# Ranks to keys with the heads innermost, a bf16 tree in place of a reduce, and another order of score and U products

## The chip, the cores and the metric

The kernel runs on one core of a Trainium2 chip. The metric is device time in microseconds, from one launch of the kernel; lower is better. Five engines work side by side, each on its own queue in order: TensorE (PE), VectorE (DVE), ScalarE (ACT), GpSimd (POOL) and SyncE (SP), which issues most of the transfers.

## What is computed

One layer of an encoder on 512 tokens of 1024 features: a mixer (a recurrence and a convolution behind one projection), then PEER, a retrieval over 128 x 128 experts, and a last norm. The change lies in PEER:

```python
def retrieve(xt):                                     # 128 tokens
    q = einsum("td,de->te", xt, w_q).reshape(128, 8, 2, 128)
    s = einsum("thpc,hpkc->thpk", q, sub_keys)        # 8 heads, 2 halves, 128 keys
    s1, i1 = top_k(s[:, :, 0], 16)
    s2, i2 = top_k(s[:, :, 1], 16)
    cand_s = s1[..., :, None] + s2[..., None, :]      # 16 x 16 pairs
    cand_i = i1[..., :, None] * 128 + i2[..., None, :]
    top_s, pos = top_k(cand_s, 16)                    # of the 256
    idx = take_along_axis(cand_i, pos)
    gate = softmax(top_s)
    act = gelu(einsum("thkd,td->thk", expert_u[idx], xt))
    return einsum("thk,thkd->td", gate * act, expert_v[idx])
```

## The kernel before

All matrix products on float32 data are made from two halves: a value is split into `hi` (a cast on ScalarE, line 108) and `lo` (a subtraction on VectorE or GpSimd, line 110), and three products are summed (`hi` by `hi`, `hi` by `lo`, `lo` by `hi`). `split` takes its buffers from a pool of three, so at most three weight tiles are split ahead of TensorE; `load` (line 101) takes one of five raw tiles of 512 KB and issues its transfer on SP's queue.

The first 128 x 3 tokens are treated densely: all 128 x 128 experts are multiplied (`u_t`, 128 chunks of U; then `v_t`, 128 chunks of V), and a gate matrix, mostly zeros, weighs them between. The last 128 tokens gather their chosen rows. The order in time is:

1. The mixer, which leaves its normed output in `m_hi` and `m_lo`, one block of 128 tokens after another (`turn`, line 134; the last block's transposes come last). A product of one U chunk (`dense_u`, line 457) reads the first 384 tokens, a query (`query`, line 562) all 512.
2. The retrieval (lines 551 to 592). For each of 16 half-heads `hp`: a query product of 24 matmuls, copied to SBUF (line 571); the scores `p_s` (line 581, eight matmul passes), copied to `s` (line 584); `rank` (line 495), five ranking instructions on VectorE for each block of 128 tokens, which leave the 16 best values and their indices in `v16` and `i16`. U products stand between them to fill TensorE: `EARLY` two ahead of the first query, one after every half-head from 1 to 14, six after the last, 22 in all. After half-heads 3, 7 and 11 `choose` (line 502) treats a pair of heads, after 13 and 15 one head.
3. `choose`: `ii` is a bf16 copy of the indices (line 510, ScalarE); the candidates' sums `cs` (line 514); their 16 best, `ts` at `pos` (line 522, two rounds of eight for each head and block); the two ranks `pb` out of the position (lines 528 to 534). Then, for each of the two keys, the index at that rank: a compare of the rank with all 16 numbers, `ioj` (line 537), a product with `ii` (line 539), and a reduce over the 16 (line 541) into `key_d`. The gates are a softmax (lines 544 to 549: GpSimd, ScalarE, VectorE, GpSimd).
4. The scatter (lines 603 to 662). `turned` (line 603) transposes gates and keys of one block, so that (head, key) lies on the partitions; for each group of `GS` = 8 tokens VectorE makes two one-hots (line 634) of the two keys and three products with the gate's three bf16 parts (line 638), and TensorE multiplies them to 128 x 128 gates a token (line 644), which go out to `scr_g` (line 648). After each 16 tokens (24 times) one more U product is made, as long as fewer than 46 are done.
5. The V stage (from line 728): each chunk of U is weighed with its gates and multiplied with its chunk of V (line 745), while the other 128 tokens' rows are gathered.

A scheduler of the framework sets the final order of instructions on each engine; instructions of neighbouring steps are seen interleaved in the trace, above all the rankings.

Of the kernel before, what the change touches and what calls it, by code (L numbers as in the profile page):

```python
# [18 lines left out]
P = 128  # L19
# [41 lines left out]
def tile_kernel(ctx, tc, x, par, wi, bd, kd, mg, wo, wq, keys, u_rows, v_rows, u_t, v_t, fg, ffg, sel, out):  # L61
# [382 lines left out]

    AHEAD_U = 51
    AHEAD_W = 2
    EARLY = 2
    us = {}

    HOMES = AHEAD_U + 1 - 8  # L450
# [26 lines left out]
    for _ in range(4):  # L477
# [21 lines left out]
    def merge(t):  # L499
        return t.rearrange("p h b k -> p (h b) k")  # L500

    def choose(rp, v, i, g, keys_, h0, n):

        hh = slice(h0, h0 + n)
        vv = v[:, hh].rearrange("p h b t k -> p (h b) t k")
        m = vv.shape[1]
        shp = [P, m, K]
        big = [P, K, m, K]
        ii = rp.tile([P, m, 2, K], BF16, name="ii")
        nc.scalar.copy(ii, i[:, hh].rearrange("p h b t k -> p (h b) t k"))  # L510

        cs = rp.tile([P, m, NCD], F32, name="cs", bufs=1)
        for lo_, ni, nj, c0 in ((0, 4, K, 0), (4, 12, 4, 64)):
            (nc.gpsimd if n > 1 else nc.vector).tensor_tensor(
                cs[:, :, c0:c0 + ni * nj].rearrange("p h (i j) -> p h i j", j=nj),
                vv[:, :, 0, lo_:lo_ + ni].unsqueeze(3).to_broadcast([P, m, ni, nj]),
                vv[:, :, 1, 0:nj].unsqueeze(2).to_broadcast([P, m, ni, nj]), op=ALU.add)
        ts = rp.tile(shp, F32, name="ts")
        pos = rp.tile(shp, U32, name="pos")
        for h in range(m):  # L520
            c2 = rp.tile([P, NCD], F32, name="c2")
            best16(ts[:, h], pos[:, h], cs[:, h], c2)

        pa = rp.tile([P, 5, m, K], U32, name="pa")
        for q, (op, arg) in enumerate(((ALU.logical_shift_right, 4), (ALU.logical_shift_right, 2),
                                       (ALU.bitwise_and, 15), (ALU.bitwise_and, 12),
                                       (ALU.logical_shift_right, 6))):
            nc.vector.tensor_scalar(pa[:, q], pos, arg, None, op0=op)
        pf = rp.tile([P, 5, m, K], F32, name="pf")
        nc.scalar.copy(pf, pa)  # L530
        pb = rp.tile([P, 2, m, K], BF16, name="pb")
        nc.vector.scalar_tensor_tensor(pb[:, 0], pf[:, 1], -12.0, pf[:, 0], op0=ALU.add, op1=ALU.max)
        nc.vector.tensor_mul(pf[:, 3], pf[:, 3], pf[:, 4])
        nc.vector.tensor_sub(pb[:, 1], pf[:, 2], pf[:, 3])
        for t in range(2):
            eq = rp.tile(big, BF16, name="eq")
            nc.vector.tensor_tensor(eq, pb[:, t].unsqueeze(1).to_broadcast(big), ioj[:, :, 0:m, :],  # L537
                                    op=ALU.is_equal)
            nc.vector.tensor_tensor(eq, eq, ii[:, :, t, :].rearrange("p h j -> p j h").unsqueeze(3)  # L539
                                    .to_broadcast(big), op=ALU.mult)  # L540
            nc.vector.tensor_reduce(merge(keys_[:, t, hh]), eq.rearrange("p j h k -> p h k j"),  # L541
                                    axis=AX.X, op=ALU.add)
        g = merge(g[:, hh])
        nc.gpsimd.tensor_tensor(g, ts, ts[:, :, 0:1].to_broadcast(shp), op=ALU.subtract)
        nc.scalar.activation(g, g, AF.Exp)
        den = rp.tile([P, m], F32, name="den")
        nc.vector.tensor_reduce(den, g, axis=AX.X, op=ALU.add)
        nc.vector.reciprocal(den, den)
        nc.gpsimd.tensor_tensor(g, g, den.unsqueeze(2).to_broadcast(shp), op=ALU.mult)

    with ExitStack() as rt:
        kp = rt.enter_context(tc.tile_pool(name="kp", bufs=1, side="right"))
        ky = kp.tile([P, 16, NK], F32, name="ky")
        nc.sync.dma_start(ky, keys)
        rp = rt.enter_context(tc.tile_pool(name="rp", bufs=2, side="right"))
        qp = rt.enter_context(tc.tile_pool(name="qp", bufs=4, side="right"))
        ps_q = rt.enter_context(tc.tile_pool(name="ps_q", bufs=3, space=PSUM))
        ps_s = rt.enter_context(tc.tile_pool(name="ps_s", bufs=3, space=PSUM))
# [44 lines left out]
    def turned(b):  # L603

        tr = bp.tile([P, P], F32, name="tr", bufs=1)
        trb = bp.tile([P, 5, P], BF16, name="trb", bufs=2)
        for dst, src in ((tr, gate_d[:, :, b]), (trb[:, 0], key_d[:, 0, :, b]), (trb[:, 1], key_d[:, 1, :, b])):
# [4 lines left out]
            nc.scalar.activation(dst, p, AF.Copy)  # L612
        for q in range(2, 5):
            nc.scalar.copy(trb[:, q], tr)
            if q < 4:
                nc.vector.tensor_sub(tr, tr, trb[:, q])
        return trb

    def scatter(b, trb):
# [3 lines left out]
        for t0 in range(0, P, GT):  # L623
            stg = bp.tile([P, NK, GT], F32, name="stg", bufs=2)
            for t1 in range(0, GT, GS):

                def over(q):
                    return (trb[:, q, t0 + t1:t0 + t1 + GS].rearrange("p (g t) -> p g t", t=SB).unsqueeze(2)
                            .to_broadcast(shp))

                hot = []
                for q in (0, 1):
                    o = bp.tile(shp, BF16, name=f"hot{q}", bufs=2)
                    nc.vector.tensor_tensor(o, iot.unsqueeze(1).to_broadcast(shp), over(q), op=ALU.is_equal)  # L634
                    hot.append(o)
                oa = bp.tile([P, 3] + shp[1:], BF16, name="oa", bufs=2)
                for q in range(3):
                    nc.vector.tensor_tensor(oa[:, q], hot[1], over(2 + q), op=ALU.mult)  # L638
                for t2 in range(0, GS, 4):
                    p = ps_g.tile([P, 4, NK], F32, name="p_g")  # L640
                    for t in range(4):
                        g, o = divmod(t2 + t, SB)
                        for q in range(3):
                            nc.tensor.matmul(p[:, t, :], hot[0][:, g, :, o], oa[:, q, g, :, o],  # L644
                                             start=(q == 0), stop=(q == 2))
                    o = t1 + t2
                    nc.scalar.activation(stg[:, :, o:o + 4], p.rearrange("p t k -> p k t"), AF.Copy)
# [213 lines left out]
```

## Time and profile before

| | us |
|---|---|
| median of 3 runs (1582.27 to 1582.92) | 1582.82 |
| the profiled execution | 1580.88 |
| its span, first to last instruction | 1579.1 |

| engine | busy us | share of the span |
|---|---|---|
| TensorE, matmuls | 1479.1 | 94% |
| TensorE, weight loads | 1299.8 | 82% |
| VectorE | 1234.1 | 78% |
| ScalarE | 634.8 | 40% |
| GpSimd | 639.4 | 40% |

Times of day are microseconds from the span's start. Busy time is an average over stages; a stage is read by its own stretch. Matmuls are pipelined and their ends are modelled, so the distance from start to start tells what one costs. "[idle before <-X]" names what ended an engine's idle time.

### The profile page before, as it was taken

Reading aid. Unit: us, or ns where it says so; the run is one execution under the profiler, and the core shown is the slowest. Engines: PE = TensorE matmul, PEld = TensorE weight load, DVE = VectorE, ACT = ScalarE, POOL = GpSimd, SP = SyncE. Lnnn points to the kernel's source line nnn. Section 1 sums busy time; section 2 is a strip of 40 time slices with the busy share of each in tenths; the row PEclk is TensorE's granted clock in tenths of the full one; section 3 lists DMA queues with packets and bytes.
Section 4 is the critical chain, followed back from the end, with each engine's and each line's share of the span. In section 5 each row is a group of like instructions: output and inputs, shape, how many; then the busy total and the mean of one; then the engine's idle time right before and its main releaser. Section 6 shows DMA issues by size and latency. Waiting matters only on the chain.

```text
span 1579.1 us, 21654 instructions
## 1 busy us (share of the span) xinstructions
PE 1479.1 (94%) x7939; PEld 1299.8 (82%) x7939; DVE 1234.1 (78%) x2304; ACT 634.8 (40%) x937; POOL 639.4 (40%) x381
## 2 busy tenths in 40 slices
PE   5987889998976999998999999999999999999997
PEld 4754757897875898997899999999999999888886
DVE  6995646389999999947777777877777777777776
ACT  5358443343333554442333333333333333333333
POOL 3644723464442000052445455545444444444440
PEclk9998879999997999999999999999999999999999
DMA  6220503322321566679999898999989988877773
GB/s 232 90 70 14 185 28 112 116 94 70 105 80 67 201 215 213 224 250 347 348 332 336 298 345 302 328 316 322 336 300 343 319 315 304 288 276 277 262 290 134
DMA packets 137787, 358.69 MB, mean 227 GB/s; under 512 B 10064, under 2 KB 59472, under 8 KB 134352
## 3 DMA queue, kind: packets, MB, share of 16 engines
q1 hardware_dynamic: 100240, 222.03, 41.3%
q0 software_dynamic: 36864, 134.23, 23.2%
q8 instruction: 62, 1.02, 0.3%
q10 hardware_dynamic: 576, 1.05, 0.2%
q14 instruction: 45, 0.37, 0.1%
HBM read 327.91 MB, written 29.36 MB: 226 GB/s over the span
## 4 chain that ended last, share of the span: by engine, by line
PE 68%; DVE 23%; issue 3%; DMA 3%; ACT 2%; POOL 1%; SPq 0%; DVEq 0%; ACTq 0%; POOLq 0%
PE po L745 31%; PE p_e L462 9%; PE p_e L464 9%; PE p_e L463 9%; DVE oa L638 2%; PE p_g L644 2%; DVE key_d L541 2%; DMA g_s<-scr_g 2%; DVE hot L634 2%; DVE w_lo L110 1%; DVE eq L539 1%; DVE eq L537 1%; DVE pc L228 1%; PE pz L417 1%; PE pz L418 1%
## 5 line engine op out<-in xcount | busy, mean ns | idle before, releaser
L108 ACT CAST w_hi<-raw_t 128x1024 fp32r<-128x1024 f32 x302 | 316.0, 1050 | 413.3 <-PE p_e L463 262.0
L462 PE MATMUL p_e<-m_hi,w_hi 128*128 128x384 f32 x1024 | 353.1, 345 | 12.1 <-ACT w_e L471 9.7
L464 PE MATMUL p_e<-m_hi,w_lo 128*128 128x384 f32 x1024 | 349.7, 342 | 6.4 <-DVE w_lo L110 6.3
L463 PE MATMUL p_e<-m_lo,w_hi 128*128 128x384 f32 x1024 | 349.4, 341 | 0.1
L110 POOL TENSOR_TENSOR w_lo<-raw_t,w_hi 128x1024 fp32r<-128x1024 f32 x73 | 194.4, 2677 | 335.0 <-ACT w_hi L108 335.0
L666 POOL DMA_INDIRECT g_t<-in_u_rows,eidx x128 | 199.9, 1562 | 226.2 <-DVE g_t L678 171.9
L110 DVE TENSOR_TENSOR w_lo<-raw_t,w_hi 128x1024 fp32r<-128x1024 f32 x229 | 276.6, 1220 | 12.4 <-ACT w_hi L108 12.4
L666 POOL DMA_INDIRECT g_t<-in_v_rows,eidx x128 | 189.9, 1484 | 224.2 <-DVE acc L688 207.8
L745 PE MATMUL po<-w_hi,wt_hi 128*128 128x512 f32 x768 | 240.7, 393 | 0.0
L745 PE MATMUL po<-w_lo,wt_hi 128*128 128x512 f32 x768 | 238.9, 390 | 0.9 <-DVE w_lo L110 0.9
L745 PE MATMUL po<-w_hi,wt_lo 128*128 128x512 f32 x768 | 239.4, 391 | 0.0
L462 PEld LDWEIGHTS p_e<-m_hi,w_hi 128*128 128x128 f32 x1024 | 196.8, 192 | 17.4 <-ACT w_e L471 11.3
L464 PEld LDWEIGHTS p_e<-m_hi,w_lo 128*128 128x128 f32 x1024 | 196.7, 192 | 7.7 <-DVE w_lo L110 7.2
L463 PEld LDWEIGHTS p_e<-m_lo,w_hi 128*128 128x128 f32 x1024 | 196.8, 192 | 3.4 <-DVE m_lo L142 0.4
L745 PEld LDWEIGHTS po<-w_lo,wt_hi 128*128 128x128 f32 x768 | 144.0, 188 | 34.6 <-DVE w_lo L110 1.8
L745 PEld LDWEIGHTS po<-w_hi,wt_lo 128*128 128x128 f32 x768 | 144.3, 188 | 30.5
L678 DVE SCALAR_TENSOR_TENSOR g_t<-g_t,Xg 128x1024 f32<-128x1024 f32 x128 | 151.9, 1222 | 16.7 <-DMA g_t<-in_u_rows,eidx 16.7
L688 DVE SCALAR_TENSOR_TENSOR acc<-g_t,dots,acc 128x1024 f32<-128x1024 f32 x127 | 162.5, 1279 | 1.6 <-DMA g_t<-in_v_rows,eidx 1.6
L745 PEld LDWEIGHTS po<-w_hi,wt_hi 128*128 128x128 f32 x768 | 143.1, 188 | 25.0 <-ACT w_hi L108 0.2
L719 ACT CAST wt_hi<-w_f 128x384 fp32r<-128x384 f32 x69 | 35.4, 513 | 183.0 <-PE po L745 183.0
L721 DVE TENSOR_TENSOR wt_lo<-w_f,wt_hi 128x384 fp32r<-128x384 f32 x69 | 38.6, 559 | 88.2 <-ACT wt_hi L719 87.8
L638 DVE TENSOR_TENSOR oa<-hot,trb 128x1024 bf16<-128x1024 bf16 x144 | 91.1, 689 | 0.0
(219 smaller groups left out, 1922.8 us busy)
## 6 DMA issues: line engine op xcount, KB each, us to landing
raw_t<-in_u_t SPq DMA_DIRECT2D x128, 512.0 KB
raw_t<-in_v_t SPq DMA_DIRECT2D x128, 512.0 KB
scr_g<-stg SPq DMA_DIRECT2D x24, 1024.0 KB
g_s<-scr_g SPq DMA_DIRECT2D x16, 1536.0 KB
raw_t<-in_wi SPq DMA_DIRECT2D x16, 512.0 KB
raw_t<-in_wq SPq DMA_DIRECT2D x16, 512.0 KB
raw_t<-in_wo SPq DMA_DIRECT2D x8, 512.0 KB
raw_t<-in_kd SPq DMA_DIRECT2D x6, 512.0 KB
```

The source lines that it names most:

```text
L108: nc.scalar.copy(hi, t)
L110: eng.tensor_sub(lo, t, f(hi))
L462: nc.tensor.matmul(p, hi[:, cs], m_hi[:, c, :TD], start=(c == 0), stop=False)
L463: nc.tensor.matmul(p, hi[:, cs], m_lo[:, c, :TD], start=False, stop=False)
L464: nc.tensor.matmul(p, lo[:, cs], m_hi[:, c, :TD], start=False, stop=(c == NC - 1))
L638: nc.vector.tensor_tensor(oa[:, q], hot[1], over(2 + q), op=ALU.mult)
L666: nc.gpsimd.indirect_dma_start(out=t, out_offset=None, in_=rows, in_offset=bass.IndirectOffsetOnAxis(ap=eidx[:, k // K, k % K:k % K + 1], ...
L678: nc.vector.scalar_tensor_tensor(t, t, 1.0, Xg, op0=ALU.mult, op1=ALU.mult, accum_out=dots[:, k:k + 1])
L688: nc.vector.scalar_tensor_tensor(acc, t, dots[:, k:k + 1], acc, op0=ALU.mult, op1=ALU.add)
L719: nc.scalar.copy(whi, flat(w))
L721: return whi, wlo, nc.vector.tensor_sub(wlo, flat(w), f(whi))
L745: nc.tensor.matmul(po[b][hf], lhs[:, bs], rhs[:, hf * 512:(hf + 1) * 512], start=(i == 0 and n == 0), stop=(i == NK - 1 and n == 2))
```

## The change

The reduce over 16 ranks in `choose` becomes a tree of adds; both keys are treated at once; the heads and blocks (`h b`, eight or four numbers) become the innermost dimension of every operand, so that `ioj`, `ii`, `pb` and `eq` are packed over (rank, head). In the loop over half-heads, the first scores stand right behind their query, ahead of query 1; one U product stands ahead of the first query and not two, none follows half-heads 0 to 2, and then as `US` says, 23 in all. In the scatter the two one-hots are made by one instruction into one tile, for which `trb` is laid out in groups of eight tokens.

```diff
-    EARLY = 2
+    EARLY = 1
+    US = (0, 0, 0, 1, 1, 2, 1, 2, 1, 2, 1, 2, 1, 2, 1, 5)
...
-    ioj = lp.tile([P, K, RM, K], BF16, name="ioj")
-    nc.gpsimd.iota(ioj, pattern=[[1, K], [0, RM], [0, K]], base=0, channel_multiplier=0,
-                   allow_small_or_imprecise_dtypes=True)
+    ioj = lp.tile([P, K, K * RM], BF16, name="ioj")
+    nc.gpsimd.iota(ioj, pattern=[[1, K], [0, K * RM]], base=0, channel_multiplier=0, allow_small_or_imprecise_dtypes=True)
...
-        ii = rp.tile([P, m, 2, K], BF16, name="ii")
-        nc.scalar.copy(ii, i[:, hh].rearrange("p h b t k -> p (h b) t k"))
+        ii = rp.tile([P, 2, K, m], BF16, name="ii")
+        nc.scalar.copy(ii, i[:, hh].rearrange("p h b t k -> p t k (h b)"))
...
-        pb = rp.tile([P, 2, m, K], BF16, name="pb")
-        nc.vector.scalar_tensor_tensor(pb[:, 0], pf[:, 1], -12.0, pf[:, 0], op0=ALU.add, op1=ALU.max)
+        pb = rp.tile([P, 2, K, m], BF16, name="pb")
+        pbm = pb.rearrange("p t k m -> p t m k")
+        nc.vector.scalar_tensor_tensor(pbm[:, 0], pf[:, 1], -12.0, pf[:, 0], op0=ALU.add, op1=ALU.max)
         nc.vector.tensor_mul(pf[:, 3], pf[:, 3], pf[:, 4])
-        nc.vector.tensor_sub(pb[:, 1], pf[:, 2], pf[:, 3])
-        for t in range(2):
-            eq = rp.tile(big, BF16, name="eq")
-            nc.vector.tensor_tensor(eq, pb[:, t].unsqueeze(1).to_broadcast(big), ioj[:, :, 0:m, :],
-                                    op=ALU.is_equal)
-            nc.vector.tensor_tensor(eq, eq, ii[:, :, t, :].rearrange("p h j -> p j h").unsqueeze(3)
-                                    .to_broadcast(big), op=ALU.mult)
-            nc.vector.tensor_reduce(merge(keys_[:, t, hh]), eq.rearrange("p j h k -> p h k j"),
-                                    axis=AX.X, op=ALU.add)
+        nc.vector.tensor_sub(pbm[:, 1], pf[:, 2], pf[:, 3])
+        eq = rp.tile([P, 2, K, K * m], BF16, name="eq", bufs=1)
+        shp2 = [P, 2, K, K * m]
+        nc.vector.tensor_tensor(eq, pb.rearrange("p t k m -> p t (k m)").unsqueeze(2).to_broadcast(shp2),
+                                ioj[:, :, 0:K * m].unsqueeze(1).to_broadcast(shp2), op=ALU.is_equal)
+        e4 = eq.rearrange("p t j (k m) -> p (t j) k m", m=m)
+        nc.vector.tensor_tensor(e4, e4, ii.rearrange("p t j m -> p (t j) m").unsqueeze(2).to_broadcast([P, 2 * K, K, m]),
+                                op=ALU.mult)
+        for w in (8, 4, 2):
+            nc.vector.tensor_add(eq[:, :, 0:w], eq[:, :, 0:w], eq[:, :, w:2 * w])
+        e1, e2 = (eq[:, :, w].rearrange("p t (k m) -> p t k m", m=m) for w in range(2))
+        nc.vector.tensor_add(keys_[:, :, hh].rearrange("p t h b k -> p t k (h b)"), e1, e2)
...
-        q = query(0)
+        qs = [query(0)]
         for hp in range(16):
-            nxt = query(hp + 1) if hp < 15 else None
+            if 0 < hp < 15:
+                qs.append(query(hp + 1))
             p = ps_s.tile([P, NB, NK], F32, name="p_s")
             for b in range(NB):
-                nc.tensor.matmul(p[:, b, :], q[:, b * P:(b + 1) * P], ky[:, hp, :], start=True, stop=True)
-            q = nxt
+                nc.tensor.matmul(p[:, b, :], qs[hp][:, b * P:(b + 1) * P], ky[:, hp, :], start=True, stop=True)
+            if hp == 0:
+                qs.append(query(1))
...
-            for _ in range(0 if hp == 0 else 6 if hp == 15 else 1):
+            for _ in range(US[hp]):
                 dense_u(len(us), nc.gpsimd)
...
-        trb = bp.tile([P, 5, P], BF16, name="trb", bufs=2)
+        trb = bp.tile([P, P // GS, 5, GS], BF16, name="trb", bufs=2)
...
-                hot = []
-                for q in (0, 1):
-                    o = bp.tile(shp, BF16, name=f"hot{q}", bufs=2)
-                    nc.vector.tensor_tensor(o, iot.unsqueeze(1).to_broadcast(shp), over(q), op=ALU.is_equal)
-                    hot.append(o)
+                hot = bp.tile([P, 2] + shp[1:], BF16, name="hot", bufs=2)
+                all_ = [P, 2 * shp[1]] + shp[2:]
+                nc.vector.tensor_tensor(hot.rearrange("p q g k t -> p (q g) k t"), iot.unsqueeze(1).to_broadcast(all_),
+                                        over(0, 2), op=ALU.is_equal)
```

## Rows read from the trace of the kernel before

**Rows 1.** Stretches: us, busy us (instructions) of PE, PEld, DVE, ACT, POOL; clock, DMA, GB/s.

```profile
268.00:503.00 235.00, 206.12 (x1047) 186.39 (x1047) 199.19 (x866) 86.01 (x125) 111.03 (x55) 0.94 0.29 97
503.00:683.00 180.00, 174.37 (x1729) 166.38 (x1730) 170.37 (x267) 88.77 (x168) 11.74 (x3) 0.97 0.56 196
735.00:1579.00 844.00, 829.60 (x4034) 736.76 (x4032) 652.80 (x841) 298.82 (x415) 382.83 (x252) 0.99 0.86 305
```

**Rows 2.** The same view, two stretches inside the retrieval.

```profile
322.00:357.00 35.00, 35.00 (x188) 31.93 (x187) 34.16 (x127) 15.02 (x21) 22.05 (x11) 1.00 0.27 93
453.00:503.00 50.00, 31.58 (x153) 29.68 (x152) 48.98 (x216) 17.65 (x27) 12.38 (x9) 0.83 0.21 71
```

**Rows 3.** Waits in the retrieval: who waited for whom, us in all, times, longest.

```profile
ACT ii L510 <- DVE i L493: 31.8, 5, 10.5
PE p_e L611 <- ACT src L610: 8.4, 1, 8.4
```

**Rows 4.** Groups by line: out<-in shapes xcount | busy us, mean ns | idle before.

```profile
L541 DVE TENSOR_REDUCE key_d<-eq 128x128 f32<-128x2048 bf16 (+1 forms) x10 | 30.8, 3081 | 0.0
L539 DVE TENSOR_TENSOR eq<-eq,ii 128x2048 bf16<-128x2048 bf16 (+1 forms) x10 | 21.0, 2099 | 0.0
L537 DVE TENSOR_TENSOR eq<-pb,ioj 128x2048 bf16<-128x2048 bf16 (+1 forms) x10 | 19.3, 1933 | 0.0
```

**Rows 5.** Timeline of VectorE in the first and last choose: start, us, engine, line.

```profile
341.03 2.28 DVE L539 TENSOR_TENSOR eq<-eq,ii 128x2048 bf16<-128x2048 bf16 x1
343.23 3.42 DVE L537 TENSOR_TENSOR eq<-pb,ioj 128x2048 bf16<-128x2048 bf16 x1
...
493.32 0.68 DVE L537 TENSOR_TENSOR eq<-pb,ioj 128x1024 bf16<-128x1024 bf16 x1
494.06 1.22 DVE L539 TENSOR_TENSOR eq<-eq,ii 128x1024 bf16<-128x1024 bf16 x1
```

**Rows 6.** Timeline of GpSimd beside the first choose, and later.

```profile
341.17 10.12 POOL L110 TENSOR_TENSOR w_lo<-raw_t,w_hi 128x1024 fp32r<-128x1024 f32 x3 [1.35 <-ACT w_hi L108]
...
362.85 2.39 POOL L110 TENSOR_TENSOR w_lo<-raw_t,w_hi 128x1024 fp32r<-128x1024 f32 x1 [3.01 <-ACT w_hi L108]
```

**Rows 7.** Timeline of TensorE: after the transposes, first query, first three scores.

```profile
275.22 0.67 PE L464 MATMUL p_e<-m_hi,w_lo 128*128 128x384 f32 x1
...
281.08 0.39 PE L567 MATMUL pq<-m_hi,w_hi 128*128 128x512 f32 x1
...
292.00 1.05 PE L581 MATMUL p_s<-ky,q 128*128 128x128 f32 x8
...
298.35 1.05 PE L581 MATMUL p_s<-ky,q 128*128 128x128 f32 x8
...
308.91 1.05 PE L581 MATMUL p_s<-ky,q 128*128 128x128 f32 x8
```

**Rows 8.** Timeline of ScalarE: a query's copy.

```profile
287.54 0.59 ACT L571 ACTIVATE q<-pq 128x512 f32<-128x512 f32 x1
```

**Rows 9.** Stretches again (columns of rows 1), around the second choose.

```profile
380.00:420.00 40.00, 35.46 (x177) 31.13 (x176) 39.93 (x163) 13.94 (x20) 18.10 (x8) 0.96 0.27 94
```

**Rows 10.** Timelines of VectorE and ScalarE: two ranks, the last rank's end, first source.

```profile
480.77 0.28 DVE L489 MAX8 v<-s 128x8 f32<-128x128 f32 x1
...
481.94 0.28 DVE L489 MAX8 v<-s 128x8 f32<-128x128 f32 x1
...
484.94 0.28 DVE L493 FIND_INDEX8 i<-v,s 128x8 uint32<-128x128 f32 x1
...
502.07 0.30 ACT L610 COPY src<-gate_d 128x128 f32<-128x128 f32 x1 [5.27 <-POOL gate_d L549]
```

**Rows 11.** Timeline of VectorE in one turn of the scatter.

```profile
615.68 1.22 DVE L110 TENSOR_TENSOR w_lo<-raw_t,w_hi 128x1024 fp32r<-128x1024 f32 x1
...
617.42 1.89 DVE L638 TENSOR_TENSOR oa<-hot,trb 128x1024 bf16<-128x1024 bf16 x3
...
622.84 1.22 DVE L110 TENSOR_TENSOR w_lo<-raw_t,w_hi 128x1024 fp32r<-128x1024 f32 x1
```

More of the change, by code (lines that the diff above doesn't have):

```diff
@@ L507, in choose @@
         shp = [P, m, K]
-        big = [P, K, m, K]
-        ii = rp.tile([P, m, 2, K], BF16, name="ii")
-        nc.scalar.copy(ii, i[:, hh].rearrange("p h b t k -> p (h b) t k"))
+        ii = rp.tile([P, 2, K, m], BF16, name="ii")
+        nc.scalar.copy(ii, i[:, hh].rearrange("p h b t k -> p t k (h b)"))
         cs = rp.tile([P, m, NCD], F32, name="cs", bufs=1)
@@ L605, in turned, with groups @@
         tr = bp.tile([P, P], F32, name="tr", bufs=1)
-        trb = bp.tile([P, 5, P], BF16, name="trb", bufs=2)
-        for dst, src in ((tr, gate_d[:, :, b]), (trb[:, 0], key_d[:, 0, :, b]), (trb[:, 1], key_d[:, 1, :, b])):
+        trb = bp.tile([P, P // GS, 5, GS], BF16, name="trb", bufs=2)
+        def groups(t):
+            return t.rearrange("p (g t) -> p g t", t=GS)
+        for dst, src in ((groups(tr), gate_d[:, :, b]), (trb[:, :, 0], key_d[:, 0, :, b]), (trb[:, :, 1], key_d[:, 1, :, b])):
             p = ps_e.tile([P, P], F32, name="p_e")
@@ L611, in turned @@
             nc.tensor.transpose(p, flat(t), ident)
-            nc.scalar.activation(dst, p, AF.Copy)
+            nc.scalar.activation(dst, groups(p), AF.Copy)
         for q in range(2, 5):
-            nc.scalar.copy(trb[:, q], tr)
+            nc.scalar.copy(trb[:, :, q], groups(tr))
             if q < 4:
-                nc.vector.tensor_sub(tr, tr, trb[:, q])
+                nc.vector.tensor_sub(groups(tr), groups(tr), trb[:, :, q])
         return trb
@@ L625, in scatter, with over @@
             for t1 in range(0, GT, GS):
-                def over(q):
-                    return (trb[:, q, t0 + t1:t0 + t1 + GS].rearrange("p (g t) -> p g t", t=SB).unsqueeze(2)
-                            .to_broadcast(shp))
-                hot = []
-                for q in (0, 1):
-                    o = bp.tile(shp, BF16, name=f"hot{q}", bufs=2)
-                    nc.vector.tensor_tensor(o, iot.unsqueeze(1).to_broadcast(shp), over(q), op=ALU.is_equal)
-                    hot.append(o)
+                def over(q, n):
+                    return (trb[:, (t0 + t1) // GS, q:q + n].rearrange("p q (g t) -> p (q g) t", t=SB).unsqueeze(2)
+                            .to_broadcast([P, n * shp[1]] + shp[2:]))
+                hot = bp.tile([P, 2] + shp[1:], BF16, name="hot", bufs=2)
+                all_ = [P, 2 * shp[1]] + shp[2:]
+                nc.vector.tensor_tensor(hot.rearrange("p q g k t -> p (q g) k t"), iot.unsqueeze(1).to_broadcast(all_),
+                                        over(0, 2), op=ALU.is_equal)
                 oa = bp.tile([P, 3] + shp[1:], BF16, name="oa", bufs=2)
                 for q in range(3):
-                    nc.vector.tensor_tensor(oa[:, q], hot[1], over(2 + q), op=ALU.mult)
+                    nc.vector.tensor_tensor(oa[:, q], hot[:, 1], over(2 + q, 1), op=ALU.mult)
                 for t2 in range(0, GS, 4):
@@ L643, in scatter @@
                         for q in range(3):
-                            nc.tensor.matmul(p[:, t, :], hot[0][:, g, :, o], oa[:, q, g, :, o],
+                            nc.tensor.matmul(p[:, t, :], hot[:, 0, g, :, o], oa[:, q, g, :, o],
                                              start=(q == 0), stop=(q == 2))
```

## The prediction

> **What bounds the kernel now.** I read the stage table first, then who waits for whom inside the retrieval, then the timelines of VectorE and TensorE. The kernel has a mixer, the retrieval (268 to 503 us), the scatter of the gates (503 to 683) and the dense V products (735 to the end). [rows 1] give each engine's busy time: in the V stage TensorE is busy 830 of 844 us, so whatever ends earlier ahead of it is kept to the end. In the retrieval VectorE is busy 199 of 235 us and TensorE 206, and neither looks like a bound until the stage is cut: in its last 50 us VectorE is busy 49 and TensorE 32, at a mean granted clock of 0.83 [rows 2]. The waits say the same: ScalarE stands 31.8 us in front of the index copy `ii` waiting for VectorE's ranks, and TensorE waits 8.4 us once for the first source of `turned` [rows 3]. So from about 321 us VectorE is last, and the others wait for it.
>
> **What a choose costs, before and after.** Lines 537, 539 and 541 take 19.3 + 21.0 + 30.8 = 71.1 us over the five calls of `choose` [rows 4]. Undisturbed prices: a bf16 product with a broadcast innermost operand takes 1.22 us for 1024 elements and 2.28 for 2048, a slope of 1.035 ns an element; a bf16 compare with packed innermost operands takes 0.68 us for 1024 [rows 5], so at half that slope (0.52 ns) 2048 elements are 1.21 us and 4096 are 2.28. The reduce over a strided axis takes 30.8 us in ten, about 3.85 for 2048, dearer still [rows 4]. After, every large operand is packed over (key, head): one compare of 4096, one product of 4096, adds of 2048, 1024 and 512, and a last add of 256 with float32 output at the full slope: 2.28 + 2.28 + 1.21 + 0.68 + 0.42 + 0.42 = 7.3 us for a pair of heads; for one head 1.21 + 1.21 + 0.68 + 0.42 + 0.29 + 0.29 = 4.1. Three and two of them: 30.1 us. VectorE loses 41 us of work, 10.6 for each pair of heads. The strided bf16 writes of `pb` (128 elements) and the permuted `ii` on ScalarE (0.4 us) have no row; between nothing and half a microsecond each, five times, under cover.
>
> The second compare of a pair took 3.42 us [rows 5]: GpSimd was then in `w_lo`, whose three took 10.1 us where one takes 2.39 [rows 6]. So compares and `w_lo` stand in each other's way, by up to one `w_lo` each time. If each of the six new instructions met a whole `w_lo`, a pair would cost 7.3 + 6 x 2.39 = 21.6 us, more than now; I take half a `w_lo` for every second one, 3.6 us, since GpSimd is busy 22 of the 35 us around the first `choose` [rows 2]: 11 us. The Trainium skill (SBUF — State Buffer, Who interferes with whom) says that a VectorE instruction with two SBUF inputs and a GpSimd instruction that reads SBUF take turns whole, and that a reduce never contends. By that rule the change replaces two reduces that were free of it by four adds that are not. The rows agree for the compares; no row shows a tree. So the rule's price is the upper one just given, 21.6 us a pair: that is the slow end of rival B.
>
> **Who is last then.** TensorE's prices are the distances of the first scores: from 292.00 to 298.35 lie one set of scores and one query, 6.35 us; from 298.35 to 308.91 the same and one U product, 10.56 us, so a U is 4.21 [rows 7]. VectorE's 199 us in the stage [rows 1] become 158, with the contention above some 11 to 15 more, 173 at most. TensorE has 16 x 6.35 + 23 x 4.21 = 198 us. So TensorE becomes the bound of the retrieval, and VectorE waits for it; and it is one in the middle too, where the new `US` puts six U products into four half-heads that hold four now: 4 x 6.35 + 6 x 4.21 = 50.7 us, in which VectorE has at most a pair's `choose` and sixteen ranks.
>
> **TensorE's sum, after.** It can go on at 275.2 us, when the last block's transposes are done (line 464 runs again there), as before. From there to the first query lay U product number two, 5.86 us, 1.65 more than its price [rows 7]: a rest of the product in front and the start at the lower clock. I keep these 1.65. Then 16 x 6.35 = 101.6 and 22 x 4.21 = 92.6 (23 in all, one ran ahead of the transposes): 194.2. New is a wait: the first scores stand behind their query's copy, and behind them on TensorE stands query 1. That copy is 0.59 us [rows 8]; with a hand-off before and after I take 1.0, between 0.6 and 1.6 (a second instruction of that length in front). Sum 275.2 + 1.65 + 194.2 + 1.0 = 472.1. The wq loads that pass U loads on SP's queue are the same 512 KB each, one for every 5 to 6 us, while the stage moves 97 GB/s where a later one moves 305 [rows 1]: nothing.
>
> To this come stalls. Around the second `choose`, from 380 to 420 us, TensorE was idle 4.5 of 40 us, and the mean granted clock of 0.96 took 1.6 more: 6.1 [rows 9]. ScalarE stood in front of `ii` and of the exponential there, waiting for a late VectorE, and the casts behind came late. The first `choose`, when VectorE was hardly late, cost TensorE nothing: from 322 to 357 us it was busy 35.0 of 35 [rows 2]. After, VectorE is not late, so I take a price near the first one's, 1 us for each of five, 5 in all (bounds 0 and 5 x 6.1 = 31). The retrieval's matmuls then end at 477.
>
> **Does VectorE's tail fit under it?** A rank of one block starts every 1.17 us (480.77, 481.94), 4.7 a half-head; from the end of the last rank (484.94) to the first source of `turned` (502.07) are 17.1 us [rows 10], less 7.5 - 4.1 = 3.4. From the last scores: about 1.0 for their copy, 4.7, 13.7 = 19.4 us. TensorE has five U products then, 5 x 4.21 = 21.0. It fits, by 1.6. So `turned(0)` starts at 477 where it started at 502.1: 25 us.
>
> **Scatter.** In a turn of 7.16 us (w_lo at 615.68 and 622.84) VectorE does ten bf16 instructions, one every 0.60 us, and one `w_lo` [rows 11]. Joining two compares of 1024: 2 x 0.60 against 0.60 + 0.53 = 1.13, a gain of 0.07, 48 times: 3.4 us. At the full slope the joined one would be 1 us dearer, 48 us in all; the instructions it joins walk the same kind of pattern at 0.60 now, which excludes that. GpSimd, which could stand in its way, has 11.7 us of work in the whole stage [rows 1]. A second loss is possible, since one tile now holds both one-hots and can be rewritten only when TensorE has read its half: 0 to 0.3 us a turn, as VectorE has the `w_lo` to do meanwhile. One U product fewer falls in the stage (23 came before it, 22 did), 1.13 us of VectorE's `w_lo` there or 4.2 of TensorE's. Both engines are near full (170 and 174 of 180 [rows 1]), so the stage gives 4 us, bounds -3 and +5. The grouped layout of `trb` changes copies of 0.3 us only.
>
> **Sum.** 25 + 4 = 29. The profiled run took 1580.88 us with a span of 1579.1; the median of the runs shown is 1582.82, 1.9 above it. Span 1550, its run 1552, median about 1554.
>
> **Rivals.**
> *A. ScalarE stays in the way.* The exponential waits for the eight rankings of candidates, which the change leaves alone; if every `choose` costs half of the dear stall, 3 us and not 1, the gain falls by 10 and more: 1560 to 1576. For it: the wait stands in the same queue. Against: the first `choose` [rows 2].
> *B. The new operations are dear* (full slope, 2 x 4.4 + 2.28 + 1.21 + 0.68 + 0.42 = 13.4 us a pair, or whole turns with GpSimd, 21.6). VectorE's stage is then 176 to 200 us; below TensorE's 198 only the tail shows, 2 to 4 us, and at 200 both are last and some 6 us more go: 1556 to 1564.
> *C. Slower.* The same queue as A at the dearest rows: each `choose` costs TensorE 6.1 us, and the tail isn't covered, so that the 8.4 us in front of `turned` [rows 3] stand again: 31 + 8 = 39 us on 472, the retrieval ends at 511, and with 4 back from the scatter the time is 1588. It decides against the change from 34 us of stalls on (30 + 4, the gain without any).
> *D. More gain:* no stall at all and the whole of the scatter's bound: 1548. Below 1545 there is no idle time of TensorE left to take in the two stages.
>
> **Chances.** Forecast (1547 to 1560) with D 0.70, A 0.16, B 0.07, C 0.04, and 0.03 for a change that ends within 0.2% because A reaches its end. About 0.2%, 3 us, is what a measurement of this kernel can tell from no change. Predicted 1554; the range goes from 1546 (D, with 2 to spare) to 1568 (half of A). Faster 0.93, within 0.2% 0.03, slower 0.04.
>
> **What would show it.** Right: line 541's reduce is gone; compare and product near 2.3 us; the first scores near 283 us, where they are at 292.0; TensorE busy nearly throughout from 276 to 477 with VectorE waiting for `s`; the first source of `turned` near 477; turns of the scatter near 7.0 us. Wrong: `ii` or the exponential on ScalarE with TensorE idle behind `w_hi`, `w_lo` or `w_e` (A, C); a compare or product of 4 us (B); joined compares over 1.35 us; a `turned` that waits for VectorE after the last U product.

## The result, and the profile after

The changed kernel takes 1564.74 us (median of 4 runs, 1563.29 to 1566.71), where the kernel before takes 1582.55 us beside it: a ratio of 0.9891, 95% interval 0.9875 to 0.9906, so 17.8 us faster. Forecast were 1554 us, a gain of 28.8. The span of the profiled run fell from 1579.1 to 1562.8 us.

Three marks cut that difference of 16.3 us: the start of the scores `p_s` of half-head 11, the first `src` of `turned`, and the span's end. Half-head 11 is the last of the third pair, behind which `choose` is called the third time.

| us | before | after | earlier or shorter |
|---|---|---|---|
| scores of half-head 11 | 410.6 | 403.9 | 6.7 |
| first `src` | 502.1 | 487.7 | 14.4 |
| between the two | 91.5 | 83.8 | 7.7 |
| from first `src` to the span's end | 1077.0 | 1075.1 | 1.9 |

The rows of these marks in the changed kernel, from the timelines of TensorE and ScalarE (start, us, engine, line):

```profile
283.93 1.16 PE L588 MATMUL p_s<-ky,q 128*128 128x128 f32 x8
294.27 1.05 PE L588 MATMUL p_s<-ky,q 128*128 128x128 f32 x8
...
403.92 1.05 PE L588 MATMUL p_s<-ky,q 128*128 128x128 f32 x8
...
487.68 0.30 ACT L623 COPY src<-gate_d 128x128 f32<-128x128 f32 x1 [3.31 <-DVE key_d L548]
```

The first scores stand at 283.93, not at 292.00 [rows 7]. From the second scores to those of half-head 11 are ten sets of scores and queries and eleven U products, by the prices of [rows 7] 10 x 6.35 + 11 x 4.21 = 109.8 us; measured are 109.65. Up to there TensorE keeps to the forecast's prices without a stall. What comes behind doesn't. The stretches of the changed kernel (us; busy us of PE, PEld, DVE, ACT, POOL; clock, DMA, GB/s):

```profile
268.00:488.00 220.00, 205.94 (x1070) 188.35 (x1068) 193.52 (x864) 87.00 (x125) 119.18 (x56) 0.95 0.30 103
404.00:487.70 83.70, 72.40 (x377) 68.51 (x375) 80.18 (x349) 34.09 (x49) 39.54 (x20) 0.90 0.25 85
440.00:490.00 50.00, 37.01 (x180) 35.01 (x179) 47.62 (x225) 20.30 (x32) 16.40 (x10) 0.83 0.25 84
```

From half-head 11 on VectorE is busy 80.2 of 83.7 us, and in the last 50 us it is busy 47.6 and TensorE 37.0, much as in [rows 2] before. The reduce is gone, but VectorE's work in the retrieval fell only from 199.2 us [rows 1] to 193.5. The groups of the new lines (retrieval; busy us, mean ns):

```profile
L546 DVE TENSOR_TENSOR eq<-eq 128x1024 bf16<-128x1024 bf16 (+3 forms) x15 | 29.3, 1956 | 0.1
L543 DVE TENSOR_TENSOR eq<-eq,ii 128x4096 bf16<-128x4096 bf16 (+1 forms) x5 | 17.3, 3457 | 0.1
L540 DVE TENSOR_TENSOR eq<-pb,ioj 128x4096 bf16<-128x4096 bf16 (+1 forms) x5 | 9.3, 1866 | 0.2
...
L548 DVE TENSOR_TENSOR key_d<-eq 128x256 f32<-128x256 bf16 (+1 forms) x5 | 4.7, 933 | 0.0
```

These make 60.6 us, against 71.1 [rows 4]: 10.5 less, not 41. The third tree (its compare, product and four adds) shows why; its rows in VectorE's timeline, without the short ranking instructions between them, then GpSimd's beside it:

```profile
424.18 2.29 DVE L540 TENSOR_TENSOR eq<-pb,ioj 128x4096 bf16<-128x4096 bf16 x1
426.60 4.28 DVE L543 TENSOR_TENSOR eq<-eq,ii 128x4096 bf16<-128x4096 bf16 x1
431.07 3.14 DVE L546 TENSOR_TENSOR eq<-eq 128x2048 bf16<-128x2048 bf16 x1
434.41 2.62 DVE L546 TENSOR_TENSOR eq<-eq 128x1024 bf16<-128x1024 bf16 x1
437.15 2.41 DVE L546 TENSOR_TENSOR eq<-eq 128x512 bf16<-128x512 bf16 x1
439.76 0.59 DVE L548 TENSOR_TENSOR key_d<-eq 128x256 f32<-128x256 bf16 x1
```

```profile
424.48 14.81 POOL L110 TENSOR_TENSOR w_lo<-raw_t,w_hi 128x1024 fp32r<-128x1024 f32 x4 [1.83 <-ACT w_hi L108]
```

An add of 512 elements takes 2.41 us where 0.42 was forecast, one of 2048 takes 3.14 instead of 1.21, and four `w_lo`, 2.39 us each when alone [rows 6], take 14.81. Product and three adds carry about 2 us each on top of the forecast's prices, the same for the long and the short: it looks as if the two engines took turns, instruction by instruction, and the experiments test that.

ScalarE's and TensorE's waits in the retrieval (us in all, times, longest), to be held against [rows 3]:

```profile
ACT ii L511 <- DVE i L494: 23.4, 5, 13.1
...
PE p_s L588 <- ACT q L577: 7.4, 1, 7.4
...
ACT src L623 <- DVE key_d L548: 3.3, 1, 3.3
```

`ii` of half-head 13 stands 13.1 us on ScalarE's queue in front of the last query's copy, and TensorE stands 7.4 us for that copy.

### The profile page after: what moved, and what is told of

It is laid out like the page before. It is cut to its first block, busy times and chain, and to the rows that moved or that the text cites. A ratio compares the mean times of both kernels' runs of the same rounds, so it can differ in the third digit from the quotient of the medians.

```text
span 1562.8 us, 21636 instructions
## 1 busy us (share of the span) xinstructions
PE 1475.6 (94%) x7939; PEld 1294.8 (83%) x7939; DVE 1230.5 (79%) x2255; ACT 636.4 (41%) x937; POOL 653.0 (42%) x382
## 4 chain that ended last, share of the span: by engine, by line
PE 77%; DVE 15%; DMA 3%; ACT 2%; issue 2%; POOL 1%; SPq 0%; DVEq 0%; ACTq 0%; POOLq 0%
PE po L758 32%; PE p_e L464 10%; PE p_e L466 10%; PE p_e L465 10%; PE p_g L657 3%; DVE oa L651 2%; DMA g_s<-scr_g 2%; PE pq L573 2%; PE pq L575 2%; PE pq L574 2%; DVE w_lo L110 1%; DVE hot L647 1%; DVE pc L228 1%; PE pz L417 1%; PE pz L331 1%
## 5 line engine op out<-in xcount | busy, mean ns | idle before, releaser
L110 POOL TENSOR_TENSOR w_lo<-raw_t,w_hi 128x1024 fp32r<-128x1024 f32 x74 | 199.0, 2703 | 344.3 <-ACT w_hi L108 331.2
L679 POOL DMA_INDIRECT g_t<-in_u_rows,eidx x128 | 210.7, 1646 | 215.4 <-DVE g_t L691 175.3
```

What stands on the lines that cost most here:

```text
L110: eng.tensor_sub(lo, t, f(hi))
L679: nc.gpsimd.indirect_dma_start(out=t, out_offset=None, in_=rows, in_offset=bass.IndirectOffsetOnAxis(ap=eidx[:, k // K, k % K:k % K + 1], ...
```

## Experiments

The theory (T in the expectations): what is missing went into turns between the tree's operations and GpSimd's `w_lo`, on VectorE, which sets the end of the retrieval. R is in each run the rival named there: that the operations are cheap and ScalarE's queue is what holds, that the two engines share by the element, that all trees count alike.

The kernels were run in three groups, each beside the kernel before on the same chip, and the ratio is to those: 1581.9 us beside e1 to e4, 1582.4 beside e5, e6, e7 and e11, 1582.85 beside e13 to e16. Marks are those of the profiled run: start of the scores of half-head 11, first `src`, the distance, and from there to the span's end. The last column differs by some 3 us between kernels that are alike there (1074.4 to 1077.7 for the changed kernel, e14 and e15), and the first scores by 2.9 us between the changed kernel and e14 (283.9 and 286.8), which are alike up to there; the distance agrees within 0.1 us.

| kernel | time (range) | ratio [95%] | half-head 11 | `src` | distance | to the end |
|---|---|---|---|---|---|---|
| before | 1582.55 (1581.15 to 1582.92) | | 410.6 | 502.1 | 91.5 | 1077.0 |
| after | 1564.74 (1563.29 to 1566.71) | 0.9891 [0.9875, 0.9906] | 403.9 | 487.7 | 83.8 | 1075.1 |
| e1_choose | 1573.35 (1570.93 to 1574.45) | 0.9948 [0.9932, 0.9965] | 407.2 | 493.0 | 85.8 | 1076.2 |
| e2_order | 1572.92 (1572.60 to 1574.46) | 0.9946 [0.9930, 0.9963] | 404.6 | 496.4 | 91.9 | 1074.4 |
| e3_hot | 1578.59 (1576.98 to 1582.07) | 0.9976 [0.9966, 0.9986] | 411.0 | 502.4 | 91.5 | 1073.9 |
| e4_no_lo | 1551.30 (1549.87 to 1554.03) | 0.9809 [0.9792, 0.9827] | 400.8 | 471.7 | 70.9 | 1077.8 |
| e5_ii_dve | 1568.80 (1566.50 to 1568.99) | 0.9909 [0.9892, 0.9925] | 405.5 | 491.7 | 86.1 | 1075.4 |
| e6_half | 1564.24 (1563.18 to 1564.93) | 0.9882 [0.9866, 0.9899] | 406.6 | 486.4 | 79.8 | 1076.7 |
| e7_quarter | 1556.70 (1555.31 to 1557.72) | 0.9839 [0.9823, 0.9856] | 402.5 | 478.1 | 75.6 | 1075.4 |
| e11_endlo | 1560.65 (1559.65 to 1563.11) | 0.9860 [0.9843, 0.9876] | 405.3 | 489.1 | 83.8 | 1072.2 |
| e14_late | 1556.82 (1555.68 to 1560.17) | 0.9839 [0.9824, 0.9854] | 406.8 | 482.4 | 75.6 | 1074.4 |
| e15_early | 1565.84 (1562.79 to 1567.75) | 0.9890 [0.9873, 0.9907] | 402.6 | 486.4 | 83.7 | 1077.7 |
| e13_quarter_end | 1553.97 (1551.48 to 1555.54) | 0.9817 [0.9803, 0.9831] | 403.1 | 478.7 | 75.6 | 1071.4 |
| e16_u_moved | 1550.98 (1548.46 to 1553.47) | 0.9796 [0.9782, 0.9809] | 401.7 | 477.0 | 75.3 | 1074.7 |

**The three parts, each alone.** The kernel before with the new `choose` only (tree, both keys at once, layouts of `ioj`, `ii`, `pb`, `eq`); with the new order of scores and U products only (`EARLY`, `US`, `qs`); with the joined one-hots only (`hot`, `trb`).

> The kernel before with the new choose alone (packed operands, tree); order of U products and one-hots as before. Theory T (VectorE's two-input operations and GpSimd's w_lo take turns, about 1.9 us a time): the five calls' compare, product and adds take near 60 us in place of 71, VectorE stays last in the retrieval, and the time falls by 8 to 12 us, to 1571-1575. Rival R (the operations are as cheap as forecast where VectorE is the bound, and the loss in the changed kernel comes from ScalarE's queue): 30 to 40 us for the five calls, the time falls by 20 or more, under 1563.

> The kernel before with the new order alone (first scores right behind their query, U products by the new list). VectorE gets its first scores 8 to 9 us earlier and is the bound from then on, so T and R both expect a gain of at most 8 us, 1574-1578; less if the later U products leave TensorE with more to do after VectorE's last rank.

> The kernel before with the joined one-hots alone. The forecast gave 3 us. By the trace after, the gain of 0.07 us per pair of compares goes again, because a product that follows right behind its own one-hot starts 1.25 us after it and not 1.14: the turn stays at 7.14 to 7.16 us and the time at 1581-1583. If the joining were worth its 0.07 us 48 times, 1579.

The new `choose` gives 8.5 us, as T has it, not the 20 and more of the rival; its operations take 58.0 us. The order alone gives 9, a little more than the 8 expected at most; its gain in the retrieval lies ahead of half-head 11 (6.1 us earlier), the distance behind stays 91.9. The joined one-hots give 3.3 us; the expectation of no change was wrong. But in the profiled runs this gain does not lie in the scatter. The first product of the V stage cuts the last column in two (TensorE's timelines of before, e3, after and e11, then the two parts):

```profile
706.85 0.39 PE L745 MATMUL po<-w_hi,wt_hi 128*128 128x512 f32 x1
707.65 0.39 PE L750 MATMUL po<-w_hi,wt_hi 128*128 128x512 f32 x1
688.81 0.39 PE L758 MATMUL po<-w_hi,wt_hi 128*128 128x512 f32 x1
687.49 0.39 PE L758 MATMUL po<-w_hi,wt_hi 128*128 128x512 f32 x1
```

| us | before | e1 | e2 | e3 | after | e7 | e11 | e13 | e16 |
|---|---|---|---|---|---|---|---|---|---|
| `src` to the first V product | 204.8 | 207.0 | 204.3 | 205.2 | 201.1 | 201.2 | 198.4 | 197.5 | 201.0 |
| from there to the end | 872.3 | 869.2 | 870.1 | 868.7 | 874.0 | 874.3 | 873.9 | 874.0 | 873.6 |

With the one-hots alone the stretch up to the V stage is 0.5 us longer, and the V stage, whose code no edit touches, 3.6 shorter; why is open. VectorE's timeline in one turn of the scatter with the one-hots alone:

```profile
562.00 1.22 DVE L110 TENSOR_TENSOR w_lo<-raw_t,w_hi 128x1024 fp32r<-128x1024 f32 x1
563.14 2.35 DVE L639 TENSOR_TENSOR hot<-iot,trb 128x2048 bf16<-128x2048 bf16 x2
565.41 3.69 DVE L643 TENSOR_TENSOR oa<-hot,trb 128x1024 bf16<-128x1024 bf16 x6
569.02 1.21 DVE L110 TENSOR_TENSOR w_lo<-raw_t,w_hi 128x1024 fp32r<-128x1024 f32 x1
```

The turn takes 7.02 us, 7.16 before [rows 11]; two joined compares start 2.27 us ahead of what follows. From the sixth turn to the last one VectorE needs 4.0 us less, but the last turn, now beside GpSimd's `w_lo`, takes 7.1 us instead of 4.3, and from `src` to the sixth turn it needs 2.8 more. Together the three would be 20.8 us, and the whole change gives 17.8.

**Is it GpSimd's `w_lo`?** First without it, in the queries and in the U products of the retrieval, where `w_hi` takes its place, so that this kernel leaves out a part of the result; then the same work in shorter instructions.

```diff
+        if eng is None:
+            return hi, hi
...
-        hi, lo = split(load(u_t[i].rearrange("p c e -> p (c e)")), eng)
+        hi, lo = split(load(u_t[i].rearrange("p c e -> p (c e)")), eng if i > 22 else None)
...
-            hi, lo = split(load(wq[hp].rearrange("p c e -> p (c e)")), nc.gpsimd)
+            hi, lo = split(load(wq[hp].rearrange("p c e -> p (c e)")), None)
```

> The changed kernel with GpSimd's w_lo left out in the retrieval: the products of the U chunks and queries there take w_hi a second time in place of w_lo, so TensorE has the same work and ScalarE too, and the values differ. T: compare and product of a pair near 2.3 us each, the five calls near 31 us, the wait of ii (23 us) under 10, TensorE's wait of 7.4 us for the query's copy gone, the first source of turned at 474-478 (487.7 with w_lo), time 1552-1556. R: the prices fall likewise, but the copy ii still holds ScalarE for 8 us or more ahead of the last queries, and the time stays over 1560.

The same operations without `w_lo` beside them (groups of the retrieval):

```profile
L548 DVE TENSOR_TENSOR eq<-eq 128x1024 bf16<-128x1024 bf16 (+3 forms) x15 | 9.6, 642 | 0.1
L542 DVE TENSOR_TENSOR eq<-pb,ioj 128x4096 bf16<-128x4096 bf16 (+1 forms) x5 | 9.3, 1866 | 0.2
L545 DVE TENSOR_TENSOR eq<-eq,ii 128x4096 bf16<-128x4096 bf16 (+1 forms) x5 | 9.3, 1854 | 0.1
...
L550 DVE TENSOR_TENSOR key_d<-eq 128x256 f32<-128x256 bf16 (+1 forms) x5 | 2.5, 502 | 0.0
```

30.7 us in all; the forecast's clean sum was 30.1. The distance falls to 70.9 us and the gain is 30.6 us, a little more than T said. Of the 40.4 us between 71.1 and 30.7, turns with GpSimd had eaten 29.9. The 71.1 were not clean either: at the prices of operations that met no `w_lo` (compare, product, reduce of a pair 1.21, 2.28, 3.85 us, of a single head 0.68, 1.22, 1.86) the three lines before would take 59 us, so some 12 were turns there too. The third tree's first and last row without `w_lo`:

```profile
421.19 2.29 DVE L542 TENSOR_TENSOR eq<-pb,ioj 128x4096 bf16<-128x4096 bf16 x1
428.86 0.58 DVE L550 TENSOR_TENSOR key_d<-eq 128x256 f32<-128x256 bf16 x1
```

The first scores come 3.8 us earlier as well (280.2), so the time of this run is not only that of the trees. A turn is in that too: an operation on one number a partition, in the norm of the last 128 tokens, takes 0.16 us here and 2.30 in the changed kernel (VectorE, first the changed kernel, then without `w_lo`):

```profile
269.29 2.30 DVE L123 TENSOR_TENSOR r_q<-r_q,r_v 128x1 f32<-128x1 f32 x1
269.09 0.16 DVE L125 TENSOR_TENSOR r_q<-r_q,r_v 128x1 f32<-128x1 f32 x1
```

The next two runs leave nothing out.

```diff
-        eng.tensor_sub(lo, t, f(hi))
+        for k in range(parts):
+            ks = slice(k * D // parts, (k + 1) * D // parts)
+            eng.tensor_sub(lo[:, ks], t[:, ks], f(hi[:, ks]))
```

> The changed kernel with GpSimd's subtraction w_lo made in two halves of 512 elements, in the retrieval and behind the scatter. T (an operation of the tree that meets GpSimd waits for one GpSimd instruction, whatever it is long): the wait in an operation falls from 1.9 us to 0.8 to 1.1, the five calls' operations from 60.6 to 44 to 50 us, first src at 478 to 482 us, time 1556 to 1560. R (they share a port by the element, so that what counts is the sum of both engines' reads): operations stay at 57 to 62 us, time 1563 to 1566.

> The changed kernel with w_lo in four parts of 256 elements. T: the wait in an operation 0.4 to 0.7 us, the five calls' operations 37 to 44 us, first src at 475 to 480 us, time 1552 to 1559, unless the fixed part of a GpSimd instruction makes the four much longer than one, by which TensorE would wait for w_lo. R (by the element): 57 to 62 us and 1563 to 1566.

The third tree with `w_lo` in four parts, on VectorE:

```profile
422.84 2.29 DVE L542 TENSOR_TENSOR eq<-pb,ioj 128x4096 bf16<-128x4096 bf16 x1
425.25 2.63 DVE L545 TENSOR_TENSOR eq<-eq,ii 128x4096 bf16<-128x4096 bf16 x1
428.07 1.48 DVE L548 TENSOR_TENSOR eq<-eq 128x2048 bf16<-128x2048 bf16 x1
429.74 0.96 DVE L548 TENSOR_TENSOR eq<-eq 128x1024 bf16<-128x1024 bf16 x1
430.82 0.75 DVE L548 TENSOR_TENSOR eq<-eq 128x512 bf16<-128x512 bf16 x1
431.77 0.86 DVE L550 TENSOR_TENSOR key_d<-eq 128x256 f32<-128x256 bf16 x1
```

The five calls take 47.3 us with halves and 37.1 with quarters, where sharing by the element would have left near 60. The turns are by instruction. In time the quarters give 8.0 us on the changed kernel, the halves only 0.5: by the time alone the halves fit R (1563 to 1566), by their operations T. Their distance falls by 4.0 us, but in that profile the first scores came 2.7 us later (286.6) and the stretch from `src` to the first V product was 1.8 longer (202.9), each within what kernels that are alike there differ by.

**Or ScalarE's queue?** `ii` is taken off it.

```diff
-        nc.scalar.copy(ii, i[:, hh].rearrange("p h b t k -> p t k (h b)"))
+        nc.vector.tensor_copy(ii, i[:, hh].rearrange("p h b t k -> p t k (h b)"))
```

> The changed kernel with the copy of the indices (ii, 5 of them) made by VectorE instead of ScalarE. T (VectorE with its turns against GpSimd is what ends last from 406 to 487 us of the changed kernel): the 13.1 us that ScalarE stood before ii and TensorE's 7.4 us before a query's copy go, but VectorE's row of work stays, longer by five copies; first src of turned at 486 to 489 us, time 1562 to 1567. R (ScalarE's queue is what costs): first src 6 to 8 us earlier, time 1556 to 1559.

Neither came out. The waits:

```profile
ACT gate_d L551 <- POOL gate_d L550: 39.1, 5, 15.1
...
PE p_s L588 <- ACT q L577: 9.7, 1, 9.7
```

The next instruction of `choose` on ScalarE, the exponential, takes `ii`'s place, waiting for the same late VectorE, and TensorE's wait grows from 7.4 to 9.7. So this run doesn't clear the queue; what it says against R is that VectorE's row, now longer (1.5 us of copies behind half-head 11, and a last add of the third tree that now meets a `w_lo`, 2.52 us instead of 0.59), made the distance 2.4 us longer and the kernel slower. The changed kernel's own trace settles it. TensorE's 7.4 us end with the last scores at 456.5, and VectorE's last pause of more than 0.2 us before `src` is the first of these, and the second is the longest behind it:

```profile
422.45 0.79 DVE L534 SCALAR_TENSOR_TENSOR pb<-pf 128x128 bf16<-128x128 f32 x1 [0.36 <-ACT pf L531]
...
480.31 0.41 DVE L534 SCALAR_TENSOR_TENSOR pb<-pf 128x64 bf16<-128x64 f32 x1 [0.19 <-ACT pf L531]
```

Scores that came sooner would have found it busy.

**Which trees count?** `w_lo` in four parts for half-heads 10 to 15 only, then for 0 to 9 only.

```diff
+            now[0] = 4 if hp >= 10 else 1
...
-            hi, lo = split(load(wq[hp].rearrange("p c e -> p (c e)")), nc.gpsimd)
+            hi, lo = split(load(wq[hp].rearrange("p c e -> p (c e)")), nc.gpsimd, parts=now[0])
```

> The changed kernel with w_lo in four parts only for the queries and U products of half-heads 10 to 15 and behind them, whole before. T (VectorE waits for the scores of half-head 11, which TensorE sets; only the trees behind them, the third pair's and the two single heads', are on the path to the scatter): from the scores of half-head 11 to the first src 76 to 78 us (83.8 in the changed kernel, 76.0 with all w_lo in four), time 1557 to 1560. R (all five trees count alike, VectorE being behind throughout): about two fifths of what all in four gave, 80 to 82 us and 1561 to 1563.

> The counterpart: w_lo in four parts for half-heads 0 to 9, whole from 10 on. T: the first two trees become 6 us shorter each and nothing follows: from the scores of half-head 11 to the first src 82 to 85 us, time 1563 to 1567. R (all trees alike): the scores or the path 4 to 5 us earlier, time 1559 to 1562.

The marks with late quarters:

```profile
406.79 1.05 PE L592 MATMUL p_s<-ky,q 128*128 128x128 f32 x8
...
482.40 0.30 ACT L628 COPY src<-gate_d 128x128 f32<-128x128 f32 x1 [3.33 <-DVE key_d L551]
```

and with early ones:

```profile
402.62 1.05 PE L592 MATMUL p_s<-ky,q 128*128 128x128 f32 x8
...
486.36 0.30 ACT L628 COPY src<-gate_d 128x128 f32<-128x128 f32 x1 [3.33 <-DVE key_d L551]
```

The distances are 75.6 us, which is all that quarters give, and 83.7, which is nothing; the times 1556.8 and 1565.8 us. The first two trees are hidden under TensorE. In the changed kernel, with halves, with quarters and without `w_lo` the compare of the third tree starts 20.3, 20.4, 20.4 and 20.4 us behind the scores of half-head 11, whatever the trees ahead took.

**The end of the scatter.** The changed kernel's `hot` and `oa` beside GpSimd's `w_lo` for the U products behind the scatter (VectorE, then GpSimd):

```profile
647.72 3.22 DVE L647 TENSOR_TENSOR hot<-iot,trb 128x2048 bf16<-128x2048 bf16 x1
...
654.04 4.04 DVE L651 TENSOR_TENSOR oa<-hot,trb 128x1024 bf16<-128x1024 bf16 x3
```

```profile
647.29 2.57 POOL L110 TENSOR_TENSOR w_lo<-raw_t,w_hi 128x1024 fp32r<-128x1024 f32 x1 [158.03 <-ACT w_hi L108]
654.30 2.64 POOL L110 TENSOR_TENSOR w_lo<-raw_t,w_hi 128x1024 fp32r<-128x1024 f32 x1 [4.44 <-ACT w_hi L108]
```

A joined compare takes 1.22 us elsewhere and three `oa` 1.90: 4.1 us of waits.

```diff
     while len(us) < AHEAD_U:
-        dense_u(len(us), nc.gpsimd)
+        dense_u(len(us), nc.vector)
```

> The changed kernel with the subtraction of the five U products behind the scatter on VectorE instead of GpSimd. T (the last groups of the scatter wait for GpSimd's w_lo at 647 and 654 us): hot and oa keep their 2.29 and 1.14 us to the end, the scatter's last product starts 3 to 4 us earlier, time 1561 to 1564. R (VectorE's five subtractions of 1.2 us come in the same place and cost as much): last product within 1 us, time 1564 to 1567.

From `src` to the first V product are 198.4 us instead of 201.1 (200.8 to 203.6 in the kernels that are alike there), and the V stage is as in the changed kernel; the time is 4.1 us lower, and the two intervals touch at 0.9875.

**Both together, and one U product moved.**

```diff
-    US = (0, 0, 0, 1, 1, 2, 1, 2, 1, 2, 1, 2, 1, 2, 1, 5)
+    US = (0, 0, 0, 1, 1, 2, 1, 2, 1, 1, 1, 2, 1, 2, 1, 6)
```

> The changed kernel with w_lo in four parts in the retrieval, and the subtractions of the five U products behind the scatter on VectorE: both edits that gave something. T (they touch different stretches): hot and oa undisturbed to the end of the scatter, path from the scores of half-head 11 as with four parts (76 us), time 1552 to 1555.5. R (four parts had already cured the end of the scatter, where oa's longest fell from 2.83 to 1.23 us): within 1 us of 1556.7.

> The same as the run with both edits, and one U product moved from behind half-head 9 to behind the last one. T (first src is the scores of half-head 11 plus a fixed path on VectorE, and TensorE idles some 7 us between 450 and 500 us): the scores of half-head 11 start 4.2 us earlier, the path stays at 75 to 77 us, first src 4 us earlier, time 3 to 4 us below the run with both edits. R (TensorE's row sets the end, so that a product moved is only put elsewhere; or VectorE is already behind at half-head 11): within 1 us of it.

Both edits together take 1554.0 us, 2.7 less than quarters alone, with intervals that overlap; from `src` to the first V product the trace has 3.7 less. With the product moved, half-head 11 comes 116.2 us behind the first scores instead of 120.4 (the 4.2 of a U product), the distance stays at 75.3, and the median falls by 3.0, with intervals that overlap a little. Most of it is given back in the trace: TensorE is in the moved product when `src` is there, so the first transpose stands 3.65 us behind `src`, where it stood 0.35 behind it, and from the first scores to the first V product the two profiled runs differ by 0.9 us only (392.5 and 393.4). So T's 3 to 4 us are not shown. At 1551.0 us this version has the lowest median of those that do all of the changed kernel's work, 13.8 us below it.

## Why the prediction was off

**Right:** that VectorE is last in the retrieval before; TensorE's sum up to half-head 11 (109.8 against 109.65 us); the clean prices of the tree (30.1 against 30.7 us); a turn of the scatter near 7.0 us, from the 15th on; the sign. The time of 1564.74 lies in the stated range of 1546 to 1568, but by luck: the upper end stood there for half of A, ScalarE's queue, and not for what happened.

**The step that failed** is the price of contention and the place where it was put. The prediction took "half a `w_lo` for every second one, 3.6 us" a pair and let it vanish, since VectorE's 173 us in the stage lay under TensorE's 198. Measured: the third pair's tree lasts 16.17 us (424.18 to 440.35), and 8.25 without `w_lo` (421.19 to 429.44): 7.9 us, in four of six operations. The first single head, which the prediction charged with nothing, lost 4.1 (8.90 us against 4.76). The rest is 0.8, together the 12.8 by which the distances 83.8 and 70.9 differ. The 41 us of work that VectorE was to lose set a clean tree against 71.1 us that held some 12 us of turns.

And it was not under cover. By the forecast VectorE had 25 us to spare over the whole stage, but they lie ahead of half-head 11. From there on TensorE has, at the prices of [rows 7], three sets of scores and queries, two scores more (0.8 us each) and eleven U products, 3 x 6.35 + 1.6 + 11 x 4.21 = 67 us, and VectorE 70.9 without contention: it is the longer of the two, and every wait is added to the time. The forecast's 477 left 73.1 us from half-head 11 on, since none of its 5 us of stalls fell ahead of it; 83.8 less 73.1 is the 10.7 us that the first `src` came late, which is the contention's 12.8 less 2.2 that VectorE had to spare against the forecast.

The tail "fits, by 1.6" failed too, hidden by those stalls. From the last scores to `src` the prediction counted 19.4 us, with one half-head to rank (0.3 of them by taking the start of the last ranking instruction, 484.94, for its end). Without `w_lo` they are 25.0 (446.6 to 471.7): VectorE is then still in the first single head's tree and has half-head 14's ranks, 4.7 us, to do before those of 15. In the changed kernel they are 29.5 (458.2 to 487.7).

**The rivals.** B named the mechanism, turns with GpSimd, and had 0.07; its 21.6 us a pair was too dear (the six operations of the third take 15.3), its "only the tail shows, 2 to 4 us" too small, and the two errors together bring the upper end of its range, 1564, close to the measured time. The rule that the prediction cited from the Trainium skill (SBUF — State Buffer, Who interferes with whom), that the two engines take turns whole, is what the traces show: the product and three adds of the third tree wait some 2 us each for a `w_lo` of 2.39, and less as it is cut shorter. The reduces that the change took out were free of it: the six of a pair took 3.78 to 3.88 us with `w_lo` beside each, twice the 1.85 of one of half the size without. A's queue was there (TensorE's 7.4 us), but VectorE had no pause longer than 0.2 us then or later. C's 31 us of stalls didn't come.

**Scatter.** Forecast 4 us, measured 3.7 from `src` to the first V product, near the number by luck: the scatter itself became longer. Its last product comes 180.2 us behind `src`, 178.0 before, mainly since GpSimd's `w_lo` took 4.1 us from VectorE at the end (177.5 with these on VectorE, e11). Behind it lie five U products and not six, 20.9 us instead of 26.8. The V stage then takes 1.7 us more, for a cause that is open, which leaves 1.9. In the kernel before, such a pair of `w_lo` came at 671 us and was itself the one that waited, 11.1 us for two. The turns also began at 7.14 us, with `hot` and `oa` alternating, and fell to 7.02 only later:

```profile
555.12 1.21 DVE L110 TENSOR_TENSOR w_lo<-raw_t,w_hi 128x1024 fp32r<-128x1024 f32 x1
556.25 1.88 DVE L651 TENSOR_TENSOR oa<-hot,trb 128x1024 bf16<-128x1024 bf16 x3
558.06 1.21 DVE L647 TENSOR_TENSOR hot<-iot,trb 128x2048 bf16<-128x2048 bf16 x1
559.31 1.90 DVE L651 TENSOR_TENSOR oa<-hot,trb 128x1024 bf16<-128x1024 bf16 x3
```

## What to carry to other kernels

Replacing one long instruction that doesn't contend by several short ones that do can cost in waits most of what it saves (29.9 of 40.4 us here): count instructions times the neighbour's instruction length, not elements. Cutting the neighbour into four gave back 8.1 of 12.8 us. Judge whether a cost is hidden from the last point at which one engine waits for the other, not over the stage: the slack ahead of that point hid the first two trees and nothing of the rest. When a wait on an in-order queue is removed, look at what stands next there.

## What the runs showed of the hardware

Here a VectorE operation on two tiles in SBUF that met GpSimd's subtraction lost 0.2 to 0.5 us less than that subtraction lasts, whatever its own size. Beside a `w_lo` of 2.39, of 1.29 (half) and of 0.74 us (quarter) an add of 2048 or 1024 elements lost 1.9, 0.84 and 0.28 us over its clean 1.21 and 0.67; the operation on one number a partition took 2.30, 1.21 and 0.66 us instead of 0.16. With work on both queues they alternate, as in the third tree. Cutting `w_lo` in four costs GpSimd 0.44 us (2.83 against 2.39 us). On VectorE an `oa` that reads the `hot` right ahead of it starts 1.25 us after the start of that `hot`; where another `hot` lies between, the two take 2.27, 1.135 each.
